# The product with w_co as seven block products instead of one full product, in an encoder layer

## The chip, the cores and the metric

The kernel runs on one NeuronCore of one Trainium2 chip. The metric is device time in microseconds (us) of one execution. Below, TensorE, VectorE (DVE), ScalarE (ACT), GpSimd (POOL) and SyncE (SP, which issues the DMAs here) are the core's engines.

## The reference

One layer of an encoder, in float32, for 1024 tokens of width 1024. Cut to what matters here:

```python
x = x + _rms_norm(mix, g_mix_post[l])
c = _memory_cross_attention(_rms_norm(x, g_cross_pre[l]), _rms_norm(mem, g_mem[l]), w_cq[l], w_ckv[l], w_co[l])
x = x + _rms_norm(c, g_cross_post[l])
f = _swiglu(_rms_norm(x, g_ffn_pre[l]), w_gate_up[l], w_down[l])
x = x + _rms_norm(f, g_ffn_post[l])

def _memory_cross_attention(h, mem_n, w_q, w_kv, w_o):
    # q (1024 tokens), k and v (256 memory tokens), 4 heads of 256
    p = jax.nn.softmax(jnp.einsum('bqhd,bkhd->bhqk', q, k) * (CROSS_HEAD_DIM ** -0.5), axis=-1)
    o = jnp.einsum('bhqk,bkhd->bqhd', p, v).reshape(b, s, D_MODEL).astype(h.dtype)
    return o @ w_o
```

The product of the change is `o @ w_o`: (1024 x 1024) times (1024 x 1024), with w_o called w_co in the kernel.

## The kernel before

Every float32 product is made of three matmuls on float32r operands: `split` (line 100) casts a value to a high part on ScalarE and subtracts that from the value on VectorE to get a low part (on GpSimd where `eng=nc.gpsimd`), and high x high, high x low and low x high are summed in PSUM. `load_w` (line 119) brings 512 KB of weights by DMA from SyncE's queue and splits them.

The kernel is written for a framework that sets the order of instructions on each engine's queue when the program is built. It takes instructions by priority, which is the order in which they are written, as far as its own estimate has them ready; work under `high_priority(AHEAD)` (AHEAD = 300) counts as written earlier. A pool hands out its buffers in the order written, and a tile's buffer is given on when its last reader is done. On the chip each queue then runs in its order.

PSUM has eight banks of 128 x 512 float32: in this part of the kernel four in pool pg, two in pn, two in px. Tokens are worked in two halves of 512 (hf 0 and 1), channels in 8 tiles of 128 (KT = 8).

The work around the change, in the order written:

1. `cross_q(hf)` (line 1116) makes the queries of a half, eight tiles of 24 matmuls in pg banks (tile pcq, line 261). `cross_attention(q)` (line 1125) goes over four heads. A head takes: the scores in two px banks (pcs, line 1137), their maximum (cmx, line 1139), the exponential (cpr, line 1144), the division by the sum (line 1147), eight transposes into two pn banks (pct, line 1153) and their split (cph, cpl), and the output in two px banks again (pco, line 1163), which is split in place over the queries. The order written is cross_q(0), cross_attention(q0), cross_q(1), cross_attention(q1).
2. `mid_gemm` (line 1034) multiplies a half by w_co: two halves of the columns, in each four loads of two weight tiles, and 96 matmuls of 512 columns over four pg banks (pmg, line 1052); 384 in all for the two halves of tokens. From each bank ScalarE takes the sum of squares (line 1055), VectorE multiplies by the gain (z, line 1056). Then come, for each of four tiles of 128 tokens, the norm's factor on GpSimd (lines 1064 and 1065), the residual (line 1066), the store to d_x2, the next norm's sum of squares and scaling (lines 1069 to 1075).
3. The scaled rows of the first half are transposed (`turned_k`, line 1191, tile ptn) and split into X11 and X21 (lines 1197 to 1200, raw copy xraw at line 1199). Those of the second half give the sums T1 to T4 and X22 (lines 1202 to 1218) for the gate/up product, which is made of seven block products in the kernel before too (as is the down projection, `block_product` at line 1400, tiles pdA, pdX, pdD).
4. The first EARLY = 4 pairs of gate/up tiles are multiplied with X11 and X21 alone (lines 1238 to 1254), while the second half is normed and transposed.

## Time and profile before

| | |
|---|---|
| time, median of 3 runs | 1535.4 us (1531.97 to 1537.91) |
| profiled execution | 1532.85 us, its span in the trace 1530.3 us |
| TensorE busy | 1484.3 us, 97% of the span |
| VectorE, ScalarE, GpSimd busy | 1068.5, 732.5, 391.2 us |
| granted TensorE clock, mean | 0.995 |

The profile is one execution. A row of groups gives line, engine, operation, output and inputs, shapes and count, then times. PE is TensorE's matmuls, PEld its weight loads. A matmul's duration in a row overlaps with its neighbours; the rate is read from long stretches. In a table of windows the columns are the window, its length, and the busy time and count of PE, PEld, DVE, ACT and (where it worked) POOL, then the granted TensorE clock, the DMA share and GB/s.

### The profile page before, as it was taken

Reading aid. Unit: us, or ns where it says so; the run is one execution under the profiler, and the core shown is the slowest. Engines: PE = TensorE matmul, PEld = TensorE weight load, DVE = VectorE, ACT = ScalarE, POOL = GpSimd, SP = SyncE. Lnnn points to the kernel's source line nnn. Section 1 sums busy time; section 2 is a strip of 40 time slices with the busy share of each in tenths; the row PEclk is TensorE's granted clock in tenths of the full one; section 3 lists DMA queues with packets and bytes.
Section 4 is the critical chain, followed back from the end, with each engine's and each line's share of the span. In section 5 each row is a group of like instructions: output and inputs, shape, how many; then the busy total and the mean of one; then the engine's idle time right before and its main releaser. Section 6 shows DMA issues by size and latency. Waiting matters only on the chain.

```text
span 1530.3 us, 21039 instructions
## 1 busy us (share of the span) xinstructions
PE 1484.3 (97%) x7451; PEld 1247.2 (81%) x7451; DVE 1068.5 (70%) x1716; ACT 732.5 (48%) x1494; POOL 391.2 (26%) x404
## 2 busy tenths in 40 slices
PE   6999999999899899999999999999999999999997
PEld 5888888877899778888887787888888888888786
DVE  6868999687789865524456387777877555696665
ACT  5678821447467664554336574323233333354532
POOL 2020221311236203243102232343434332000021
PEclk9999999999999999999999999999999999999999
DMA  6235575856997684453213354343433334853355
GB/s 208 76 108 149 145 194 150 217 167 176 313 315 221 200 280 155 150 168 106 76 54 132 111 192 131 125 137 116 160 124 104 103 104 168 291 178 98 104 177 167
DMA packets 264709, 242.95 MB, mean 159 GB/s; under 512 B 33800, under 2 KB 203677, under 8 KB 264605
## 3 DMA queue, kind: packets, MB, share of 16 engines
q1 hardware_dynamic: 264605, 241.62, 50.4%
q8 instruction: 58, 0.95, 0.3%
q14 instruction: 46, 0.38, 0.1%
HBM read 172.07 MB, written 66.88 MB: 156 GB/s over the span
## 4 chain that ended last, share of the span: by engine, by line
PE 75%; DVE 10%; DMA 6%; ACT 4%; issue 2%; SPq 2%; POOL 1%; DVEq 0%; POOLq 0%; ACTq 0%
PE pmg L1052 10%; PE pD L1231 8%; PE pE L1231 8%; PE pA L1231 7%; PE pcq L261 6%; PE pdX L1421 6%; PE pg L261 5%; PE pdA L1421 4%; PE pB L1231 4%; PE psc L809 3%; PE pdX L1514 2%; PE pdD L1421 2%; DVE acc L286 2%; PE pcs L1137 1%; PE pco L1163 1%
## 5 line engine op out<-in xcount | busy, mean ns | idle before, releaser
L103 ACT CAST whi<-wraw 128x1024 fp32r<-128x1024 f32 x108 | 113.4, 1051 | 160.5 <-PE pmg L1052 34.4
L261 PE MATMUL pg<-hhi,whi 128*128 128x512 f32 x352 | 139.3, 396 | 0.0
L261 PE MATMUL pg<-hlo,whi 128*128 128x512 f32 x352 | 139.3, 396 | 0.0
L261 PE MATMUL pg<-hhi,wlo 128*128 128x512 f32 x352 | 138.3, 393 | 0.0
L104 POOL TENSOR_TENSOR wlo<-wraw,whi 128x1024 fp32r<-128x1024 f32 x38 | 91.8, 2415 | 178.7 <-ACT whi L103 178.7
L104 DVE TENSOR_TENSOR wlo<-wraw,whi 128x1024 fp32r<-128x1024 f32 x70 | 88.6, 1266 | 69.8 <-ACT whi L103 65.8
L1052 PE MATMUL pmg<-whi,b 128*128 128x512 f32 x384 | 119.2, 394 | 0.4 <-ACT b L103 0.4
L1231 PE MATMUL pA<-s,whi 128*128 128x512 f32 x352 | 109.4, 392 | 1.0 <-ACT m L1248 1.0
L1052 PEld LDWEIGHTS pmg<-whi,b 128*128 128x128 f32 x384 | 71.4, 188 | 15.4 <-ACT b L103 1.3
L1421 PE MATMUL pdX<-dhl,whi 128*128 128x512 f32 x264 | 76.1, 390 | 1.5 <-DVE zv L1476 0.7
L1231 PEld LDWEIGHTS pA<-s,whi 128*128 128x128 f32 x352 | 65.5, 188 | 14.7 <-ACT m L1248 1.5
L261 PEld LDWEIGHTS pg<-hhi,whi 128*128 128x128 f32 x352 | 66.4, 189 | 13.4 <-ACT hhi L103 0.2
L261 PEld LDWEIGHTS pg<-hhi,wlo 128*128 128x128 f32 x352 | 66.5, 189 | 12.8
L261 PEld LDWEIGHTS pg<-hlo,whi 128*128 128x128 f32 x352 | 66.3, 188 | 12.8
L1308 POOL TENSOR_TENSOR act<-act,up 128x512 f32<-128x512 f32 x33 | 50.1, 1517 | 89.6 <-DVE up L1307 53.1
L1052 PE MATMUL pmg<-wlo,b 128*128 128x512 f32 x192 | 71.9, 391 | 0.0
L103 ACT CAST whi<-araw 128x1024 fp32r<-128x1024 f32 (+1 forms) x36 | 35.3, 981 | 71.3 <-PE pdX L1421 27.6
L1231 PE MATMUL pA<-s,wlo 128*128 128x512 f32 x176 | 68.7, 391 | 0.1
L104 DVE TENSOR_TENSOR wlo<-araw,whi 128x1024 fp32r<-128x1024 f32 (+1 forms) x36 | 40.8, 1132 | 38.9 <-ACT whi L103 38.8
L286 DVE SCALAR_TENSOR_TENSOR acc<-cp,cols,acc 128x1024 f32<-128x1024 f32 x48 | 62.0, 1293 | 0.1
L1280 POOL TENSOR_TENSOR sr<-wraw 128x512 f32<-128x512 f32 x22 | 30.0, 1362 | 125.2 <-DMA wraw<-in_w_gate_up_dram 125.2
L1451 POOL TENSOR_SCALAR frs<-sq 128x1 f32<-128x1 f32 x8 | 12.0, 1498 | 195.4 <-ACT jk L1440 194.5
(415 smaller groups left out, 4113.1 us busy)
## 6 DMA issues: line engine op xcount, KB each, us to landing
wraw<-in_w_gate_up_dram SPq DMA_DIRECT2D x52, 512.0 KB, 3.8
kv<-d_kv SPq DMA_DIRECT2D x32, 512.0 KB, 7.4
wraw<-in_w_in_dram SPq DMA_DIRECT2D x22, 512.0 KB, 4.5
b<-in_w_down_dram SPq DMA_DIRECT2D x20, 512.0 KB, 7.3
araw<-d_as SPq DMA_DIRECT2D x20, 512.0 KB, 3.9
pz<-d_pz SPq DMA_DIRECT2D x32, 256.0 KB, 6.7
wraw<-in_w_ckv_dram SPq DMA_DIRECT2D x16, 512.0 KB, 5.4
wraw<-in_w_out_dram SPq DMA_DIRECT2D x16, 512.0 KB, 3.7
```

What stands on the lines that cost most here:

```text
L103: nc.scalar.copy(hi, src)
L104: (eng or nc.vector).tensor_tensor(lo, src, f32(hi), ALU.subtract)
L261: nc.tensor.matmul(p_, w[:, k, :], ah[a][:, k, :], start=(k == 0 and i == 0), stop=(k == nk - 1 and i == 2))
L286: nc.vector.scalar_tensor_tensor(acc, cp[:, t:t + S], taps[t], acc, ALU.mult, ALU.add)
L809: nc.tensor.matmul(out[:, d, h, :], lt[:, d, h, :], rt[:, d, h, :], start=True, stop=True)
L1052: nc.tensor.matmul(pp[t], act[a][:, k, tt], w_[:, kk, :], start=(k == 0 and i == 0), stop=(k == KT - 1 and i == 2))
L1137: nc.tensor.matmul(pp[:, t2_, :], q[a][:, ct, tt], kr_[b_][:, ct, :], start=(j == 0 and i == 0), stop=(j == 1 and i == 2))
L1231: nc.tensor.matmul(out_, w[a][:, k, :], xx[b_][:, k, :], start=(start and k == 0 and i == 0), stop=(k == HK - 1 and i == 2), skip_group_ch ...
L1280: nc.gpsimd.tensor_tensor(s[0], b_[:, 0:HK], b_[:, HK:], ALU.add)
L1308: nc.gpsimd.tensor_tensor(o_, o_, up, ALU.mult)
L1421: nc.tensor.matmul(banks[t], a[:, k - k0, tt], w, start=(first and k == 0 and i == 0), stop=(k == NB - 1 and i == 2), skip_group_check=not ...
L1514: nc.tensor.matmul(X[t], a[:, k], w[:, k0 + k], start=False, stop=(k0 + k == NB - 1 and i == 2), skip_group_check=True)
```

## The change

With the attention's outputs (tokens by channels) in blocks A11, A12 (first half of tokens, first and second half of channels), A21, A22 (second half of tokens) and w_co in blocks B11, B12, B21, B22, the product is made of seven block products, each of 4 x 4 x 3 = 48 matmuls:

- A11 B11 and A12 B21, whose sum is the first half's left columns; the first is also kept as p1;
- S2 (B22 - B12 + B11), S1 (B12 - B11), S4 B22 and S3 (B22 - B12), and A22 (B21 - (B22 - B12 + B11)),

with S1 = A21 + A22, S2 = S1 - A11, S3 = A11 - A21, S4 = A12 - S2. The other three blocks of the result are sums of p1 and these on VectorE. The sums of weights are made on GpSimd (`minus`), those of attention outputs on VectorE out of the output banks, with float32 copies of the first half's outputs (raw) made by ScalarE. The first two products, S4's weights and the loads of blocks (`load_block`) use 14 loads of 512 KB. Products A11 B11, A12 B21, S4, S3 and A22 use pg banks, S2 and S1 the two px and the two pn banks. The norm of the first rows (`finish`) is written beside S3's product, their transposes after A22's; the buffers of several tiles move.

The core of the diff; left out are the pools' places, the transposes' sources and the names of X22's buffer:

```diff
-    def cross_attention(q):
+    def cross_attention(q, hf):
         for h in range(4):
             prs = []
             mxs = tx.tile([P, 4], F32, tag="cmx", name="cmx")
@@ -1162,47 +1167,199 @@
                     for i, (a, b_) in enumerate(((0, 0), (0, 1), (1, 0))):
                         nc.tensor.matmul(po, vr_[a][:, kt, cs], pts[kt][b_], start=(kt == 0 and i == 0),
                                          stop=(kt == 1 and i == 2))
-                split(q[0][:, 2 * h + j, :], q[1][:, 2 * h + j, :], po)
+                ct = 2 * h + j
+                if hf == 0:
+                    nc.scalar.copy(raw[:, ct], po)
+                    split(q[0][:, ct, :], q[1][:, ct, :], po)
+                    continue
+                k = ct % (KT // 2)
+                if ct < KT // 2:
+                    nc.scalar.copy(s1_[:, k], po)
+                    d_ = rg.tile([P, HALF], F32, tag="wpart", name="cs3", bufs=7)
+                    nc.vector.tensor_tensor(d_, raw[:, k], po, ALU.subtract)
+                    split(q[0][:, k], q[1][:, k], d_)
+                    continue
+                split(q[0][:, ct, :], q[1][:, ct, :], po)
+                nc.vector.tensor_tensor(s1_[:, k], s1_[:, k], po, ALU.add)
+                nc.vector.tensor_tensor(raw[:, k], s1_[:, k], raw[:, k], ALU.subtract)
+                nc.vector.tensor_tensor(raw[:, ct], raw[:, ct], raw[:, k], ALU.subtract)
 
     q0 = cross_q(0)
-    cross_attention(q0)
+    cross_attention(q0, 0)
     q1 = cross_q(1)
-    cross_attention(q1)
+    HK = KT // 2
+    wco = [opA.tile([P, KT, HALF], F32, tag=f"s0{i}", name="wco") for i in range(2)]
+    (b1_, b12), (b2_, p1_) = ((t[:, 0:HK], t[:, HK:KT]) for t in wco)
+
+    def load_block(b_, i, j):
+        for k0 in (0, 2):
+            nc.sync.dma_start(b_[:, k0:k0 + 2], w_co[(HK * i + k0) * P:(HK * i + k0 + 2) * P, j * HALF:(j + 1) * HALF]
+                              .rearrange("(k p) n -> p k n", p=P))
+
+    for b_, i, j in ((b12, 0, 1), (b1_, 0, 0), (b2_, 1, 1)):
+        load_block(b_, i, j)
+    cross_attention(q1, 1)
...
+    def weight_part(b_, k):
+        with tc.high_priority(AHEAD):
+            dh, dl = (rg.tile([P, HALF], F32R, tag="wpart", name="wpart", bufs=7) for _ in range(2))
+            split(dh, dl, b_[:, k])
+        return dh, dl
+
+    def act_part(a, k0):
+        if isinstance(a, tuple):
+            return [h[:, k0:k0 + 2] for h in a]
+        with tc.high_priority(AHEAD):
+            ah, al = (wp.tile([P, 2, HALF], F32R, tag=t, name=t) for t in ("whi", "wlo"))
+            split(ah, al, a[:, k0:k0 + 2])
+        return ah, al
+
+    def three(bank, ah, al, dh, dl, tt, start, stop, check):
+        for i, (a, w) in enumerate(((ah, dh), (ah, dl), (al, dh))):
+            nc.tensor.matmul(bank, a[:, tt], w, start=(start and i == 0), stop=(stop and i == 2), skip_group_check=not check)
+
+    def block_product(banks, a, b_, first=True, last=True, extra=None):
+
+        for k in range(HK):
+            if k % 2 == 0:
+                ah, al = act_part(a, k)
+            if isinstance(b_, tuple):
+                if k % 2 == 0:
+                    wh, wl = load_w(w_co[(HK * b_[0] + k) * P:(HK * b_[0] + k + 2) * P, HALF * b_[1]:HALF * (b_[1] + 1)], 2, HALF)
+                dh, dl = wh[:, k % 2], wl[:, k % 2]
+            else:
+                dh, dl = weight_part(b_, k)
+            for t in range(4):
+                three(banks[t], ah[:, k % 2], al[:, k % 2], dh, dl, slice(t * P, (t + 1) * P), first and k == 0,
+                      last and k == HK - 1, first and last)
+            if extra:
+                extra(k)
+
+    def minus(o_, a, b_):
+        nc.gpsimd.tensor_tensor(o_, a, b_, ALU.subtract)
+
+    def square_of(src, ch, r):
+        jk = tz.tile([P, D], F32, tag="junk", name="junk")[:, 0:src.shape[-1]]
+        nc.scalar.activation(jk, src, AF.Square, accum_out=ssq[:, ch, r:r + 1])
+
+    def finish(r, parts, eng):
+
+        tok = slice(r * P, (r + 1) * P)
+        xr = tz.tile([P, D], F32, tag="xr", name="xr", bufs=2)
+        nc.sync.dma_start(xr, d_x1[tok, :])
+        rs = tz.tile([P, 1], F32, tag="prs", name="prs", bufs=4)
+        nc.gpsimd.tensor_scalar(rs, ssq[:, 1, r:r + 1], ssq[:, 0, r:r + 1], D * EPS, ALU.add, ALU.add)
+        nc.gpsimd.tensor_tensor(rs, rs, mhalf[:, 0:1], ALU.pow)
+        for z, o_ in parts:
+            c_ = slice(o_, o_ + z.shape[-1])
+            nc.vector.scalar_tensor_tensor(xr[:, c_], z, rs, xr[:, c_], ALU.mult, ALU.add)
+        nc.sync.dma_start(d_x2[tok, :], xr)
+        s2 = tz.tile([P, 1], F32, tag="ps2", name="ps2", bufs=4)
+        jk = tz.tile([P, D], F32, tag="junk", name="junk")
+        nc.scalar.activation(jk, xr, AF.Square, accum_out=s2)
+        r2 = tz.tile([P, 1], F32, tag="pr2", name="pr2", bufs=4)
+        rstd_of(r2, s2, 1.0 / D, EPS)
+        for z, o_ in parts:
+            c_ = slice(o_, o_ + z.shape[-1])
+            if eng is nc.scalar:
+                nc.scalar.activation(z, xr[:, c_], AF.Identity, scale=r2)
+            else:
+                nc.vector.tensor_scalar(z, xr[:, c_], r2, None, ALU.mult)
+
+    a11, a12, s3_, a22 = ((q_[0][:, c], q_[1][:, c]) for q_ in (q0, q1) for c in (slice(0, HK), slice(HK, KT)))
+    s2_, s4_ = blocks(raw)
+
+    def four(spec):
+        return [p_.tile([P, HALF], F32, tag=t_, name="pst") for p_, t_ in spec]
+
+    def sums(k):
+        minus(b1_[:, k], b12[:, k], b1_[:, k])
+        minus(b12[:, k], b2_[:, k], b12[:, k])
+        minus(b2_[:, k], b2_[:, k], b1_[:, k])
+
+    A = four([PG] * 4)
+    block_product(A, a11, (0, 0), last=False)
+    for t in range(4):
+        nc.scalar.copy(p1_[:, t], A[t])
+    block_product(A, a12, (1, 0), first=False, extra=sums)
+    X = four([PX] * 2 + [PN] * 2)
+    block_product(X, s2_, b2_, last=False)
+    for t in range(4):
+        nc.scalar.activation(zz[:, t, 0:HALF], A[t], AF.Square, accum_out=ssq[:, 0, t:t + 1])
+        nc.vector.tensor_tensor(zz[:, t, 0:HALF], A[t], gp[:, 0:HALF], ALU.mult)
+    Y = four([PG] * 4)
+    block_product(Y, s4_, (1, 1))
+    for t in range(4):
+        nc.vector.tensor_tensor(zv[:, t], p1_[:, t], X[t], ALU.add)
+    block_product(X, s1_, b1_, first=False)
+    load_block(b1_, 1, 0)
+    for t in range(4):
+        nc.vector.tensor_tensor(zz[:, t, HALF:], p1_[:, t], Y[t], ALU.add)
+    for t in range(4):
+        nc.vector.tensor_tensor(zz[:, t, HALF:], zz[:, t, HALF:], X[t], ALU.add)
+        nc.vector.tensor_tensor(za[:, t], p1_[:, t], X[t], ALU.add)
+        square_of(zz[:, t, HALF:], 1, t)
+    Y = four([PG] * 4)
+    block_product(Y, s3_, b12, last=False, extra=lambda k: minus(b1_[:, k], b1_[:, k], b2_[:, k]))
+    for t in range(4):
+        nc.vector.tensor_tensor(zz[:, t, HALF:], zz[:, t, HALF:], gp[:, HALF:], ALU.mult)
+        finish(t, [(zz[:, t], 0)], nc.scalar)
+    for t in range(4):
+        nc.vector.tensor_tensor(za[:, t], za[:, t], Y[t], ALU.add)
+        square_of(za[:, t], 1, 4 + t)
+        nc.vector.tensor_tensor(za[:, t], za[:, t], gp[:, HALF:], ALU.mult)
+    acts = [act_part(a22, k0) for k0 in (0, 2)]
+    wts = [weight_part(b1_, k) for k in range(HK)]
+    for t in range(4):
+        for k in range(HK):
+            ah, al = (h[:, k % 2] for h in acts[k // 2])
+            three(Y[t], ah, al, *wts[k], slice(t * P, (t + 1) * P), False, k == HK - 1, False)
+        nc.vector.tensor_tensor(zv[:, t], zv[:, t], Y[t], ALU.add)
+        square_of(zv[:, t], 0, 4 + t)
+        nc.vector.tensor_tensor(zv[:, t], zv[:, t], gp[:, 0:HALF], ALU.mult)
+        finish(4 + t, [(zv[:, t], 0), (za[:, t], HALF)], nc.vector)
...
```

More of the change, by code (lines that the diff above doesn't have):

```diff
@@ L1175, in tile_hybrid_block @@
     opC = LX.enter_context(pool("opC", 1))
-    X22 = [opC.tile([P, KT // 2, HALF], F32R, name=f"x22{i}") for i in range(2)]
+    zz = opC.tile([P, 4, D], F32, tag="x22", name="zz")
     L3 = ExitStack()
-    tr = L3.enter_context(pool("tr", 1))
-    raw = tr.tile([P, KT, HALF], F32, name="xraw")
-    tz = L3.enter_context(pool("tz2", 1, side="right"))
+    tz = L3.enter_context(pool("tz2", 1))
     gp = gpost_tile(tz, g_cross_post)
-    HK = KT // 2
+    za, zv = (tz.tile([P, 4, HALF], F32, name=n) for n in ("za", "zv"))
@@ L1184, in blocks @@
+    ssq = tz.tile([P, 2, NT], F32, name="ssq")
     def blocks(t):
         return t[:, 0:HK], t[:, HK:KT]
[L1187 to L1188 removed]
+    def weight_part(b_, k):
[10 more added lines that the diff above has]
+        return ah, al
@@ L1203, in tile_hybrid_block @@
+    T2, T4 = (blocks(t) for t in operand(opA, "s0"))
     T1, T3 = (blocks(t) for t in operand(opB, "s2"))
+    X22 = opC.tile([P, 2, HK, HALF], F32R, tag="x22", name="x22")
+    X22 = [X22[:, i] for i in range(2)]
     for k in range(HK):
-        p0, p1 = turned_k(xn, k), turned_k(xn, k + HK)
+        p0, p1 = turned_k(last_rows, k), turned_k(last_rows, k + HK)
         g0, g1 = gain("ffn", k), gain("ffn", k + HK)
```

25 lines of the change are left out of this document (17 added, 8 removed).

## The prediction

> **What bounds the kernel now.** I read the page's engine totals and its chain first, then windows around the product with w_co, then single rows of the cross-attention beside it.
>
> ```profile
> PE 1484.3 (97%) x7451; PEld 1247.2 (81%) x7451; DVE 1068.5 (70%) x1716; ACT 732.5 (48%) x1494; POOL 391.2 (26%) x404
> ```
> ```profile
> PE 75%; DVE 10%; DMA 6%; ACT 4%; issue 2%; SPq 2%; POOL 1%; DVEq 0%; POOLq 0%; ACTq 0%
> ```
>
> TensorE is busy 97% of the span and is three quarters of the chain that ended last. A busy share alone says little of matmuls that overlap, so the rate comes next, from the chain in order of time: a stretch of the down projection, which already runs as seven block products.
>
> ```profile
> 1370.48 29.92 PE pdD L1421 x132
> ```
>
> A 512-column matmul costs 29.92/132 = 0.2267 us when nothing interrupts. A matmul removed is worth 0.2267 us only where TensorE has no other wait, so the idle time around the change decides. From the windows (the second column is the length, the third TensorE's busy time):
>
> ```profile
> 777.80:853.00 75.20, 72.61 (x378) 60.55 (x378) 43.24 (x69) 38.56 (x86) 9.81 (x16) 1.00 0.26 91
> ...
> 853.00:943.00 90.00, 87.19 (x406) 70.34 (x405) 60.02 (x78) 53.75 (x94) 25.34 (x26) 1.00 0.49 164
> ```
>
> The first window is the second half's cross-attention, the second is the rest of the w_co stage with the early gate/up products. TensorE idles 2.59 us in the one and 2.81 us in the other. So the w_co matmuls are paid in full, and there are only 5.4 us of waits for the change to remove. Why does an attention that is a chain of small steps leave TensorE busy? The windows of the w_co product alone (tile pmg) answer:
>
> ```profile
> 686.50:777.80 91.30, 17.62 (x72) 13.30 (x72) 0.00 (x0) 0.00 (x0) 1.00 0.30 95
> 777.80:853.00 75.20, 47.12 (x193) 35.41 (x194) 5.39 (x8) 5.39 (x16) 1.00 0.26 91
> 853.00:884.00 31.00, 29.05 (x120) 21.88 (x120) 4.00 (x6) 4.76 (x15) 1.00 0.42 136
> ```
>
> Of the 384 matmuls, 72 lie beside the first half's attention and 193 beside the second half's. They are the cover of the attention.
>
> **The change, term by term.** Removed: 384 matmuls become 7 x 4 x 4 x 3 = 336. That is 48 x 0.2267 = 10.9 us less on a full TensorE.
>
> Now the cover. The first two products (a11, a12) need only the first half's attention outputs, and they are 96 matmuls. Before, all 192 of the first half and those of the second half's finished heads could be used. The products with s2, s4 and s1 need all of the second half but for a part: the first half of s4's product (24 matmuls) after the third head. X's banks are the attention's own px and pn. The rows of the heads:
>
> ```profile
> 738.49 3.04 PE L1137 MATMUL pcs<-kr,b 128*128 128x256 f32 x24
> ...
> 761.72 3.04 PE L1137 MATMUL pcs<-kr,b 128*128 128x256 f32 x24
> ...
> 779.06 1.59 PE L1137 MATMUL pcs<-kr,b 128*128 128x256 f32 x12
> ...
> 801.15 3.04 PE L1137 MATMUL pcs<-kr,b 128*128 128x256 f32 x24
> ...
> 807.25 0.69 DVE L1147 TENSOR_TENSOR cpr<-cpr,csum 128x512 f32<-128x512 f32 x1
> ...
> 832.47 1.03 PE L1153 MATMUL pct<-ident,cpr 128*128 128x128 f32 x8
> ...
> 839.23 1.59 PE L1137 MATMUL pcs<-kr,b 128*128 128x256 f32 x12
> ...
> 852.28 0.40 PE L1163 MATMUL pco<-cph,vr 128*128 128x512 f32 x1
> ```
>
> While cover lasts a head takes 17 to 23 us (738.49 to 761.72 to 779.06), as the queue's order has it. The last head, with little cover, takes 852.68 - 839.23 = 13.4 us. TensorE's own part of a head is 24 score matmuls (3.04), 8 transposes (1.03) and 12 output matmuls (12 x 0.2267 = 2.72), 6.8 us. The first half's attention is placed after the same query projections as before, so I take it to use the same 72 matmuls, now of the 96. For the second half's heads 24 are left, and the 24 of s4: 48 x 0.2267 = 10.9 us. Four heads take 4 x 13.4 = 53.6 us and hold 4 x 6.8 + 10.9 = 38.1 us of work: 15.5 us idle where 2.6 us stood, +12.9 us. Bounds: heads of 11.5 us with their steps closer, or 14.5 us with more queued behind them: +6 to +18 us.
>
> Extra readers of the attention's output banks. Each bank is now also copied (first half, ScalarE) or added (second half's last two heads, VectorE) before the next head's scores may take it:
>
> ```profile
> L103 ACT CAST b<-pco x16: 568/587/593, 709.5 to 852.7; 128x512 fp32r<-128x512 f32 x16
> L104 DVE TENSOR_TENSOR b<-pco,b x16: 680/691/692, 710.1 to 853.5; 128x512 fp32r<-128x512 f32 x16
> ```
>
> One of a head's two banks is on the way to the next head: 4 x 0.587 + 2 x 0.691 = 3.7 us. In the first half this is not idle time but cover spent early, which is missing later. Bounds: 0 if the queue hides it, 7.5 us for both banks.
>
> The end of the attention. X may start when the last output bank is free: cast, subtraction, addition, 0.587 + 2 x 0.691 = 2.0 us. Bounds: 0, if s4's 24 matmuls are kept for it, and 6 us with three more subtractions and the split of s2.
>
> The clock. This case's trace has one place where TensorE waits a little in the middle of work:
>
> ```profile
> 535.93 0.38 PE L654 MATMUL psw<-khi,qs 128*128 128x256 f32 x1 [2.15 <-DVE m L656]
> ```
> ```profile
> 536.00:538.00 2.00, 1.66 (x9) 1.32 (x10) 1.80 (x7) 0.97 (x3) 0.20 (x1) 0.73 1.03 388
> 538.00:540.00 2.00, 2.00 (x9) 1.52 (x7) 0.58 (x3) 2.00 (x10) 0.00 (x0) 0.50 1.05 395
> 540.00:542.00 2.00, 1.77 (x7) 1.04 (x7) 1.91 (x7) 1.96 (x4) 0.00 (x0) 0.92 1.07 376
> ```
>
> After 2.15 us of idle the granted clock was 0.73, 0.50 and 0.92 in three stretches of 2 us, which loses 2 x (0.27 + 0.50 + 0.08) = 1.7 us of full speed. A naked head has one longer gap, from the last score matmul (804.19) to the end of the softmax (807.94), 3.75 us. Two of the four heads stay without cover in it: 2 x 1.7 = 3.4 us; bounds 0 and 13.6 us (two gaps in every head).
>
> [...]
>
> After the attention. Five products, TensorE has 4 x 48 + 24 matmuls, 49 us, and beside them stand many reads of banks and splits:
>
> ```profile
> L1056 DVE TENSOR_TENSOR z<-pmg,gpost x32: 676/684/693, 575.5 to 886.2; 128x512 f32<-128x512 f32 x32
> ```
> ```profile
> L104 DVE TENSOR_TENSOR wlo<-wraw,whi 128x1024 fp32r<-128x1024 f32 x70 | 88.6, 1266 | 69.8 <-ACT whi L103 65.8
> ...
> L1280 POOL TENSOR_TENSOR sr<-wraw 128x512 f32<-128x512 f32 x22 | 30.0, 1362 | 125.2 <-DMA wraw<-in_w_gate_up_dram 125.2
> ...
> wraw<-in_w_out_dram SPq DMA_DIRECT2D x16, 512.0 KB, 3.7
> ```
> ```profile
> 812.82 1.28 DVE L1066 SCALAR_TENSOR_TENSOR z<-z,prs,xr 128x1024 f32<-128x1024 f32 x1 [0.36 <-POOL prs L1065]
> ...
> 817.40 1.14 ACT L1075 ACTIVATE xr<-z,pr 128x1024 f32<-128x1024 f32 x1
> ```
> ```profile
> L1199 ACT ACTIVATE xraw<-ptn,cols x8: 689/701/735, 853.2 to 868.7; 128x512 f32<-128x512 f32 x8
> ```
>
> VectorE: 32 operations on banks and sums and 16 weight splits at 0.69 (33 us), 8 splits at 1.27 (10 us), four residual updates at 1.28 (5 us): 48 us in 49 us, if none is done ahead. It is nearly full. The first rows' norm and turning, before under the last 120 matmuls, now start when s1's product ends, under 96 (21.8 us). In the old rows the residual update to the scaled row is 818.54 - 812.82 = 5.7 us, three more tiles two ScalarE passes of about 1.14 us each, 6.8 us, and the turning 15.5 us from 853.2 to 868.7, of which the early gate/up products need the first half before they start: 5.7 + 6.8 + 7.8 = 20 us at best, 28 us for all. I take 3 us, bounds 0 and 8 us.
>
> Hidden: the twelve and four weight subtractions on GpSimd (16 x 1.36 = 22 us) lie beside the attention, where GpSimd has 9.81 us of work in 75; without that cover s2's product would wait for them. The w_co loads are 14 of 512 KB instead of 16; the six that now stand on SP's queue ahead of the second attention wait for the end of the query projection, and take 6 x 3.7 = 22 us at most, where s2's product comes a whole attention (53.6 us) later. The eight fp32 copies of the first half and four of the second are on ScalarE, busy 38.56 of 75.20 us; their part on the banks is counted above. The last rows' norm goes on under the same early products as before, at no change.
>
> Sum: -10.9 + 12.9 + 3.7 + 2.0 + 3.4 + 3 = +14.1 us. The profiled execution took 1532.85 us (span 1530.3), so 1547.0 us for it; on the median of the three runs, 1535.4 us, it is 1549.5 us, the forecast. Half a percent, about what a measurement of this kernel can tell from no change, is 7.7 us: 1527.7 and 1543.1.
>
> **The rivals.** *The cover lasts.* If the queue's order spends fewer matmuls on the first half's heads, with three of them at 17.3 us (the step 761.72 to 779.06) instead of 23.2, 18 us of the 96 matmuls' cover move to the second half and the 15.5 us of idle time vanish, the clock term with them. What is left is -10.9 - 2.6 + 3.7 + 2.0 and nothing after: -7.8, 1528 us; 1524 if the banks cost nothing. For it: 17.3 occurred. Against: the same projections lie beside the same heads, and the 72 matmuls were spent there. It decides when the idle time of the whole stage stays under 8.6 us (5.4 + 10.9 - 7.7).
>
> *Half covered.* If also X's part on the two pn banks fills the last heads (12 to 24 matmuls, 2.7 to 5.4 us) and the clock stays up, +14.1 - 5.4 - 3.4 = +5.3, 1541 us. For it: pn is free once the last head is transposed. Against: X's px half waits for the last bank.
>
> *The clock falls in every head.* Two gaps in each of four heads: 8 x 1.7 instead of 3.4, +24.3 us, 1560 us. For it: the wait for the transposed probabilities' split is a second gap. Against: that split's first part should take about the 0.59 us of the same cast on an output bank.
>
> *VectorE bounds the five products.* The 8 us bound in place of 3, with 6 at the attention's end: +23.1, 1558.5 us. Against: loads of weights and b2's splits can be done in the attention.
>
> **How the numbers follow.** Forecast 0.46 (its own range 1540 to 1562), cover lasts 0.22, half covered 0.16, clock 0.09, VectorE 0.07. Faster by over 0.5%: 0.20, nearly all of the first rival. Within: 0.24, half covered, a tail of the forecast and the first rival's weaker end. Slower: 0.56, the rest. The range 1526 to 1570 leaves out the best end of the first rival (0.08) and sums where several upper bounds meet (0.1).
>
> **What would show it.** The w_co product has 336 matmuls. Right: the second half's heads come every 12 to 15 us and TensorE idles 12 to 20 us in them, with the granted clock under 1.00 there; the first output product is finished before the third of these heads; the last products run at 0.2267 us with under 6 us of waits. Wrong: heads of 17 us and more with TensorE full to the end of the attention (then it is faster), or idle time mostly behind the attention, named by VectorE.

## The result, and the profile after

The changed kernel takes 1579.5 us (median of 4 runs, 1577.3 to 1583.1), the kernel before 1536.5 us in the same comparison: 1.0287 times as long, 95% interval 1.0255 to 1.0320. That is 43 us more where the forecast was 14 more. It was slower, as forecast, but by three times as much.

The profiled execution of the changed kernel took 1581.4 us, its span is 1579.7 us. Its page, engine totals and the chain that ended last:

```profile
PE 1491.0 (94%) x7403; PEld 1245.9 (79%) x7403; DVE 1108.9 (70%) x1776; ACT 747.2 (47%) x1522; POOL 414.6 (26%) x420
```
```profile
PE 40%; DVE 1%; POOL 1%; ACT 1%; issue 0%; DVEq 0%; POOLq 0%; ACTq 0%
```

The 48 matmuls are gone (7403 instead of 7451), but TensorE is busy longer, 1491.0 us instead of 1484.3: the mean granted clock of this execution was 0.984, before 0.995. Its share fell from 97% to 94%. The chain, followed back from the end, now gets no further than the stage of the change.

The loss is all in one place. From the start to the first score matmul of the cross-attention (655.5 us before, 656.4 after) and from the first pB matmul (the early product that needs the last rows' sums) to the end (597.8 and 598.9 us) the two kernels agree. Between them I cut three stretches: the second half's attention (from 777.8 us in every run) up to its last output matmul, then the products up to the last w_co matmul, then the stretch from there to the first pB matmul, called the tail below. Windows of the kernel before (start and end, length, TensorE's busy time, then the other engines; the number ahead of the DMA share is the granted clock):

```profile
777.80:852.60 74.80, 72.22 (x374) 60.15 (x374) 43.10 (x68) 38.16 (x85) 9.81 (x16) 1.00 0.27 92
852.60:882.80 30.20, 30.20 (x148) 25.07 (x147) 10.90 (x13) 18.38 (x36) 12.19 (x13) 1.00 0.39 129
882.80:932.50 49.70, 48.62 (x226) 39.07 (x224) 43.65 (x58) 34.62 (x57) 13.16 (x14) 1.00 0.54 182
```

The same three stretches of the changed kernel:

```profile
777.80:837.60 59.80, 43.25 (x211) 33.94 (x210) 32.14 (x62) 23.17 (x60) 2.52 (x3) 0.89 0.00 1
837.60:909.00 71.40, 60.77 (x242) 46.71 (x241) 49.52 (x66) 33.80 (x57) 18.23 (x20) 0.93 0.35 118
909.00:980.80 71.80, 55.28 (x252) 43.04 (x250) 54.57 (x75) 45.98 (x83) 23.24 (x26) 0.92 0.46 154
```

The attention ends 15 us earlier, because fewer product matmuls lie in it. But the products behind it take 71.4 us, of which 240 x 0.2267 = 54.4 us are TensorE's own work, and the tail takes 71.8 us instead of 49.7. TensorE is idle 59.80 - 43.25 = 16.6, then 10.6 and 16.5 us: 43.7 us instead of 2.6 + 0 + 1.1 = 3.7. The granted clock, 1.00 before, is 0.89, 0.93 and 0.92; length times what is missing to 1 gives 6.6 + 5.0 + 5.7 = 17.3 us. That is an estimate, since it takes in the idle time too; by busy time it is 19.2 us (159.3 us instead of 151.0, with 10.9 us of work gone). Together: -10.9 + 40.0 + 17.3 = 46.4 us, against 203.0 - 154.7 = 48.3 us by the windows.

The table of waits says for whom TensorE waited (the changed kernel from 777.8 to 985 us: sum, times, longest, in us):

```profile
PE pct L1158 <- DVE cpr L1152: 10.9, 6, 3.9
PE pB L1388 <- ACT s1h L103: 8.6, 1, 8.6
PE pst L1233 <- ACT whi L103: 5.8, 4, 2.1
PE pst L1233 <- DVE wlo L104: 2.4, 3, 1.3
PE ptn L1343 <- DVE zv L1281: 2.4, 1, 2.4
PE ptn L1343 <- ACT zz L1279: 2.3, 1, 2.3
PE pcs L1142 <- DVE cs L1179: 1.9, 2, 0.9
...
PE pcs L1142 <- DVE os L1183: 1.5, 1, 1.5
```

The first is the wait for a head's softmax, now with nothing beneath it, the second the tail, the third and fourth the splits of the products' operands. The largest of the kernel before in the same place (777.8 to 935 us):

```profile
PE pA L1231 <- ACT m L1248: 1.0, 1, 1.0
```

### The profile page after: what moved, and what is told of

The parts are those of the page before. It is cut to its first block, busy times and chain, and to the rows that moved or that the text cites. A ratio compares the mean times of both kernels' runs of the same rounds, so it can differ in the third digit from the quotient of the medians.

```text
span 1579.7 us, 21087 instructions
## 1 busy us (share of the span) xinstructions
PE 1491.0 (94%) x7403; PEld 1245.9 (79%) x7403; DVE 1108.9 (70%) x1776; ACT 747.2 (47%) x1522; POOL 414.6 (26%) x420
## 5 line engine op out<-in xcount | busy, mean ns | idle before, releaser
L103 ACT CAST whi<-wraw 128x1024 fp32r<-128x1024 f32 x98 | 102.9, 1051 | 153.4 <-DMA wraw<-in_w_gate_up_dram 30.4
L1388 PE MATMUL pA<-b,whi 128*128 128x512 f32 x352 | 112.7, 400 | 3.5 <-ACT m L1405 1.9
L104 DVE TENSOR_TENSOR wlo<-wraw,whi 128x1024 fp32r<-128x1024 f32 x60 | 77.7, 1296 | 44.7 <-ACT whi L103 42.1
L1388 PEld LDWEIGHTS pA<-b,whi 128*128 128x128 f32 x352 | 66.4, 191 | 18.4 <-ACT m L1405 2.3
L261 PEld LDWEIGHTS pg<-hhi,wlo 128*128 128x128 f32 x352 | 66.2, 188 | 12.8
L261 PEld LDWEIGHTS pg<-hlo,whi 128*128 128x128 f32 x352 | 66.2, 188 | 12.8
L1388 PE MATMUL pA<-b,wlo 128*128 128x512 f32 x176 | 69.3, 394 | 0.0
L1388 PE MATMUL pB<-s,s1h 128*128 128x512 f32 x176 | 54.8, 393 | 8.6 <-ACT s1h L103 8.6
L1579 PEld LDWEIGHTS pdX<-dhl,whi 128*128 128x128 f32 x264 | 49.3, 188 | 12.8 <-ACT dhl L103 1.1
L103 ACT CAST dhl<-b 128x512 fp32r<-128x512 f32 x66 | 40.4, 620 | 33.5 <-PE pdA L1579 14.1
```

Of the source, the lines that this page charges most:

```text
L103: nc.scalar.copy(hi, src)
L104: (eng or nc.vector).tensor_tensor(lo, src, f32(hi), ALU.subtract)
L261: nc.tensor.matmul(p_, w[:, k, :], ah[a][:, k, :], start=(k == 0 and i == 0), stop=(k == nk - 1 and i == 2))
L1388: nc.tensor.matmul(out_, w[a][:, k, :], xx[b_][:, k, :], start=(start and k == 0 and i == 0), stop=(k == HK - 1 and i == 2), skip_group_ch ...
L1579: nc.tensor.matmul(banks[t], a[:, k - k0, tt], w, start=(first and k == 0 and i == 0), stop=(k == NB - 1 and i == 2), skip_group_check=not ...
```

## The experiments

Times are medians with their range. Each ratio is to the kernel before, run beside it (its medians there: 1535.4 for the first four, 1535.0 for the next four, 1536.0 for e9 to e12, 1532.9 for e13 and e14). The changed kernel's own ratio is 1.0287 [1.0255, 1.0320], so a change to it of under some 6 us can't be told from none. The windows and waits of a run are those of its one profiled execution.

**More cover, placed first (e1).** A11 x B11 is made twice:

```diff
     A = four([PG] * 4)
+    block_product(A, a11, (0, 0), last=False)
     block_product(A, a11, (0, 0), last=False)
```

> The changed kernel with the product of the blocks A11 and B11 made twice (the second time over the first): 48 more matmuls of 512 columns, 10.9 us at 0.2267 us each, that need only the first half's attention. Theory (the second half's attention has too little cover, and its waits let the clock fall): they go into waits that are there anyway, the time rises by 0 to 4 us or falls, and the second half's heads up to the second show TensorE full at clock 1.00. Rival (TensorE's own work bounds the stage): plus 10.9 us, ratio to the kernel before up by 0.007.

Measured: 1587.0 us (1585.6 to 1588.6), 1.0329 [1.0312, 1.0346]. That is 7 us more than the changed kernel for 10.9 us of added work, between the two expectations, and the intervals do not tell it from the whole 10.9. The last heads stayed bare: TensorE still waits 10.5 us for softmaxes in this attention (10.9 in the changed kernel), and its end moved out by 8 us.

**Four buffers for the residual rows (e2).** Each row from the third on gets memory of its own, in blocks that are dead by then:

```diff
-        xr = tz.tile([P, D], F32, tag="xr", name="xr", bufs=2)
+        if r < 2:
+            xr = tz.tile([P, D], F32, tag="xr", name="xr", bufs=2)
+        else:
+            xr = (s1_, b2_, b12)[r // 2 - 1][:, r % 2 * 2:r % 2 * 2 + 2].rearrange("p k n -> p (k n)")
```

> The changed kernel with no residual tile used again: rows 0 and 1 keep their two buffers, rows 2 to 7 take blocks that are dead by then (S1, the weight sums). Theory A (two residual buffers in turn hold up the norms of the rows, first the first rows' transposes, then the last rows', until the early gate/up products run out): 15 to 22 us faster, the wait of 8.6 us before the first product with T2 gone or under 2 us. Theory B (VectorE's and GpSimd's own work in that tail is the bound): under 4 us faster, the wait moves little.

Measured: 1582.3 us (1576.5 to 1584.5), 1.0292 [1.0266, 1.0318]: no change. The theory that the two row buffers by themselves set the tail fell.

**S4's product ahead of S2's (e3).** Two statements change places, so that S4's 48 matmuls, which need no bank of the attention, come first:

```diff
+    Y = four([PG] * 4)
+    block_product(Y, s4_, (1, 1))
     X = four([PX] * 2 + [PN] * 2)
     block_product(X, s2_, b2_, last=False)
...
-    Y = four([PG] * 4)
-    block_product(Y, s4_, (1, 1))
```

> The changed kernel with S4's product written before S2's. As it is, S4's splits take the two buffers of weight parts behind those of S2's second half, which is ready only at the attention's end, so its first 24 matmuls covered nothing. Theory (order of the buffers): 24 matmuls of S4 lie before the attention's end and the time falls by 4 to 8 us. Rival (S4's sums are ready too late or VectorE is full): within 2 us.

Measured: 1582.6 us (1578.9 to 1584.8), 1.0298 [1.0277, 1.0318]: no change. S4's product did not move beneath the attention. TensorE's waits in this run have a new line:

```profile
PE pst L1233 <- DVE zz L1301: 6.2, 1, 6.2
```

S4's pg banks hold the first output block. That is evacuated into zz with the gain, and by the order of the kernel's pools both lie in memory that comes free only when the attention is over.

**Low parts of the weight sums on GpSimd (e4).**

```diff
-            split(dh, dl, b_[:, k])
+            split(dh, dl, b_[:, k], eng=nc.gpsimd)
```

> The changed kernel with the low parts of the 16 weight-sum splits on GpSimd in place of VectorE: 16 x 0.69 = 11 us less on VectorE, 16 x 1.3 = 21 us more on GpSimd, which is nearly idle from the second half's attention to its end. Theory (VectorE bounds the five products and lengthens the heads): 4 to 8 us faster. Rival (TensorE waits there for the order of buffers and the clock): within 2 us, or slower by up to 5 us because each split takes twice as long.

Measured: 1580.7 us (1580.0 to 1584.1), 1.0286 [1.0268, 1.0304]. The products behind the attention took 67.0 us instead of 71.4, and the tail 75.0 instead of 71.8. The first of these is no sure gain: in e1, e5 and e7, where nothing of these five products was changed, they took 67.5 to 67.9 us. The expected 4 to 8 us did not come.

**A scratch tile of its own for the second sum of squares (e5), the same with e2 (e6).** The squares of `finish` no longer share the tile "junk" with those of `square_of`:

```diff
-        jk = tz.tile([P, D], F32, tag="junk", name="junk")
+        jk = p1_[:, r % 2 * 2:r % 2 * 2 + 2].rearrange("p k n -> p (k n)")
```

> The changed kernel with the scratch output of the second sum of squares of each row tile put in the dead block p1, so that the one buffer of the scratch tile is left to the first sums of squares. Theory (the buffer is handed out in the order written, so the square of row tile t+1's product waits for tile t's whole norm, and the last four tiles come 6 to 9 us apart where they came 1.5 us apart before): the last four scalings come within 12 us instead of 18.9, and the time falls by 6 to 15 us. Rival (the order on VectorE and GpSimd or the two residual buffers hold them as much): within 3 us.

> The changed kernel with both: the scratch in p1 and no residual tile used again. Theory (two chains of buffers in series, each hiding the other's removal): 12 to 20 us faster than the changed kernel, the 8.6 us wait before the first T2 product under 3 us. Rival (VectorE and GpSimd are the bound of that tail): under 5 us faster.

Measured: 1577.0 us (1573.0 to 1580.1), 1.0267 [1.0235, 1.0299], and 1577.0 us (1575.9 to 1578.4), 1.0268 [1.0238, 1.0299]: two or three us, which the intervals do not tell from none. But the two edits together did what neither did alone. The last four scalings lay 18.4 us apart, first to last start, in the changed kernel, 17.3 in e2 and 22.0 in e5 (12 were expected); in e6 they lie 6.0 us apart, close to the 5.4 of the kernel before. The first and the last of them:

```profile
924.24 1.49 DVE L1284 TENSOR_SCALAR zv<-wco,pr 128x512 f32<-128x512 f32 x1
...
930.22 1.50 DVE L1284 TENSOR_SCALAR zv<-wco,pr 128x512 f32<-128x512 f32 x1 [0.44 <-POOL pr L162]
```

So the row buffer and the scratch tile space the last rows, each of them enough by itself; and the spacing is not what sets the tail, which is 69.0 us long in e6 instead of 71.8. The sums T1 to T4 began 14 us earlier, but the first pB matmul came only 2.7 us earlier. TensorE's waits of e6 from 900 to 985 us, the first two:

```profile
PE ptn L1346 <- DVE zv L1284: 6.8, 1, 6.8
PE pB L1391 <- ACT s1h L103: 2.0, 1, 2.0
```

The wait for pB fell from 8.6 to 2.0 us, and one of 6.8 us for the last rows' scaled values stands in its place: their transposes are ahead of early products on TensorE's queue.

**The cover spread over the heads (e7), and e2, e5 and e7 together (e8).** Groups of the first two products are held behind the scores of later heads; a pair in `hold` names the half and the head, one for each of a product's four groups:

```diff
+                if hold and hold[k]:
+                    order_.enter_context(tc.issue_after(last_score[hold[k]].ins))
...
-    block_product(A, a11, (0, 0), last=False)
+    block_product(A, a11, (0, 0), last=False, hold=(None, None, (1, 0), (1, 0)))
...
-    block_product(A, a12, (1, 0), first=False, extra=sums)
+    block_product(A, a12, (1, 0), first=False, extra=sums, hold=((1, 1), (1, 1), (1, 2), (1, 3)))
```

> The changed kernel with the matmuls of A11 B11 and A12 B21 held back: 24 free, 24 behind the scores of the second half's first head, 24 behind the second's, 12 behind the third's and 12 behind the fourth's. The number of matmuls is the same. Theory (the cover is spent in the first half's heads, and each naked head idles about 4 to 6 us and lets the clock fall): TensorE's idle time in the second half's attention falls from 16.7 us to under 9, the clock stays at 1.00 there, the time falls by 7 to 14 us. Rival (the first half's last head loses as much as the others gain): within 3 us.

> The changed kernel with the scratch in p1, no residual tile used again, and the cover held back. If attention and tail are separate losses, the gains add: 20 to 32 us faster than the changed kernel, 1548 to 1560 us. If the time lost is one shared bound (VectorE over the whole stage), the sum is much less than the parts: under 12 us.

Measured: e7 1579.2 us (1575.5 to 1581.3), 1.0280 [1.0252, 1.0308]; e8 1574.2 us (1571.0 to 1576.7), 1.0249 [1.0221, 1.0277]. In e7 the waits in the attention did shrink and its clock stayed at 1.00 (below, under the hardware), and the last w_co matmul came 6.8 us earlier. But the profiled execution was e7's fastest, 1575.5 us, and the median did not move. All three together won at most some 5 us where 20 to 32 were expected if attention and tail were separate losses; the interval overlaps with the changed kernel's. Mending the changed kernel wait by wait does not find the loss. The next runs test the order of the work.

**The kernel before in the changed kernel's order (e9).** The full product, no block sums; only the first half's first columns lie beneath the second attention, and the first rows' result is whole 96 matmuls ahead of the last rows'. In `chunk` the arguments are the operand, the half of the rows, the half of the columns, the banks, and the matmul behind which it is held:

```diff
-    xn = mid_gemm(tz, q0, w_co, gp, d_x1, d_x2, 0)
+    chunk(q0, 0, 0, [PG] * 4)
+    chunk(q1, 1, 0, [PX] * 2 + [PN] * 2)
+    chunk(q0, 0, 1, [PG] * 4, last_pco)
+    xn = norm_rows(0)
+    chunk(q1, 1, 1, [PG] * 4)
...
-    xn = mid_gemm(tz, q1, w_co, gp, d_x1, d_x2, 1, vec=True)
+    xn = norm_rows(1)
```

> The kernel before, with the full product and no block sums, but in the order of the changed kernel: only the first half's first 512 columns (96 matmuls) are made beneath the second half's attention; the second half's first columns, the first half's last columns and the second half's last columns follow it, so that the first rows' result is whole 96 matmuls before the last rows' instead of about 240. Theory (the loss comes from giving up the stagger of the two halves): the second attention ends 10 to 16 us earlier, the stretch from the last product matmul to the first early product grows from 49.7 to 60 or more, and the kernel takes 1565 to 1590 us. Rival (the loss comes from the extra sums, splits and bank readers of the seven products): only the missing cover in the attention is felt, that stretch stays at 47 to 53 us, and the kernel takes 1545 to 1555 us.

Measured: 1568.1 us (1566.4 to 1571.5), 1.0209 [1.0180, 1.0238]. The order, with the banks and buffers that it needs (px and pn banks for one block, the last rows' block in the later memory of X22) and none of the change's arithmetic, costs 32 us. The three stretches:

```profile
777.80:837.40 59.60, 45.42 (x226) 35.29 (x225) 28.25 (x54) 21.00 (x59) 0.00 (x0) 0.91 0.05 18
837.40:900.70 63.30, 63.30 (x283) 52.40 (x282) 26.52 (x28) 28.40 (x47) 11.74 (x21) 1.00 0.47 156
900.70:966.30 65.60, 55.55 (x253) 43.22 (x251) 48.22 (x59) 43.52 (x73) 23.00 (x22) 0.95 0.41 135
```

The attention and the tail look like those of the changed kernel (14.2 and 10.1 us idle). The products do not: with the full product TensorE is busy all of 63.3 us at full clock. The longest of TensorE's waits from 895 to 970 us are for the first rows' splits and raw copies (s, xraw) and for a weight split:

```profile
PE pA L1286 <- POOL s L104: 2.3, 2, 2.1
PE pA L1286 <- ACT whi L103: 2.1, 1, 2.1
PE ptn L1247 <- ACT xraw L1252: 1.9, 1, 1.9
```

**Only the cover taken away (e13).** The kernel before, its order kept, but the first half's last columns held behind the attention:

```diff
+                    if ch and hold is not None:
+                        order_.enter_context(tc.issue_after(hold.ins))
...
-    xn = mid_gemm(tz, q0, w_co, gp, d_x1, d_x2, 0)
+    xn = mid_gemm(tz, q0, w_co, gp, d_x1, d_x2, 0, hold=last_pco)
```

> The kernel before, with the full product, where the first half's last 512 columns (96 matmuls) are held behind the second half's last attention output and everything else keeps its order: the cover in the attention is that of the changed kernel (96 matmuls), but the first rows' result is still whole 192 matmuls before the last rows'. It parts the 32 us of the run without the stagger into the missing cover and the nearness of the two results. If the missing cover alone costs them: 1564 to 1572 us. If the nearness of the two norms counts by itself: the attention's idle time and lowered clock stay (about 14 and 5 us), the stretch from the last product to the first early product is back at 50 to 55 us, and the kernel takes 1550 to 1560 us.

Measured: 1554.4 us (1551.9 to 1558.4), 1.0137 [1.0106, 1.0167].

```profile
777.80:837.60 59.80, 47.04 (x210) 36.23 (x209) 28.51 (x54) 20.62 (x59) 0.00 (x0) 0.80 0.06 18
837.60:908.50 70.90, 69.82 (x322) 57.45 (x321) 26.80 (x28) 36.99 (x63) 22.55 (x29) 1.00 0.41 141
908.50:958.10 49.60, 48.51 (x226) 39.11 (x225) 43.52 (x58) 34.55 (x57) 13.11 (x14) 1.00 0.52 176
```

The attention still lacks its cover (12.8 us idle, clock 0.80), but with 192 matmuls between the two results the tail is 49.6 us, that of the kernel before (49.7). So e13 and e9 part the 32 us: some 21 for the missing cover, lowered clock included, some 11 for two results that come close together (by the two intervals 5 to 17).

**Norms left out of the changed kernel (e10, e11, e14).** `finish` is taken out for the last rows, for the first rows, or for both, and a store of the columns with their gain stands in its place, so these kernels leave out the norm, the residual and its load.

> The changed kernel with the last rows' norm and residual left out (their scaled columns are stored and turned as they are); the products, the bank sums and the first rows' norm stay. Theory (the stretch after the last product is set by the last rows' norm, whose rows follow each other at 6 to 7 us): 15 to 22 us less, 1557 to 1564 us. Rival (the first rows' turning and its splits set that stretch): 0 to 5 us less, 1574 to 1579 us.

> The changed kernel with the first rows' norm and residual left out (their scaled columns are stored and turned as they are); the last rows' norm stays. Theory (two norms at the same time hold each other up on VectorE, ScalarE and GpSimd): the last rows follow each other at 2 to 3 us, 10 to 20 us less, 1559 to 1569 us. Rival (the last rows' own chain is what takes the time, alone as well): 0 to 5 us less, 1574 to 1579 us.

> The changed kernel with both norms and residuals left out (all scaled columns are stored and turned as they are); products and bank sums stay. If the two norms hold each other up and nothing else: the gains of the two runs with one norm left out (8.2 and 13.9 us) add up or more, 1550 to 1558 us. If behind them the next wait is as long (bank sums, turning): 1560 to 1567 us.

Measured: 1571.3 us (1566.6 to 1572.0), 1565.6 us (1564.0 to 1570.1) and 1561.8 us (1560.9 to 1562.6); ratios 1.0220 [1.0195, 1.0246], 1.0195 [1.0169, 1.0220], 1.0182 [1.0152, 1.0211]. Without the last norm 8 us are won and without the first 14, the one between its two expectations, the other in the theory's; without both it is no more than 18, the second expectation. The tail goes from 71.8 us to 61.3, 60.3 and 53.0 us. The windows of e14:

```profile
777.80:843.30 65.50, 49.20 (x229) 38.66 (x228) 34.36 (x65) 23.82 (x62) 5.83 (x4) 0.84 0.03 9
843.30:909.10 65.80, 58.23 (x259) 45.70 (x258) 46.34 (x64) 32.20 (x60) 12.88 (x8) 1.00 0.31 104
909.10:962.10 53.00, 49.54 (x234) 39.78 (x233) 41.64 (x57) 34.74 (x60) 8.67 (x6) 1.00 0.45 147
```

(The first score matmul of e14 came 3.5 us later than the changed kernel's, so its first stretch begins that much earlier in the work.) Without norms the tail is nearly that of the kernel before: each norm taken out shortens it by about 10 us. But the kernel before has the last rows' norm in its tail of 49.7 us too. With that norm alone, in e11, the tail is still 60.3 us, 10.6 us longer, with the first rows' transposes and splits left in it. So a second norm is about half of what lengthens the tail; the rest these runs do not part. What still costs in e14 is the attention (16.3 us idle) and the products (7.6 us). One part of the theory fell: the slow last rows were read as held up by the first rows' norm. Scaling of the last rows, in the kernel before, in the changed one, and in e11 (four operations; first and last start):

```profile
L1073 DVE TENSOR_SCALAR xr<-z,pr x4: 752/753/756, 888.5 to 893.9; 128x1024 f32<-128x1024 f32 x4
```
```profile
L1281 DVE TENSOR_SCALAR zv<-xr,pr x4: 483/489/496, 923.2 to 941.6; 128x512 f32<-128x512 f32 x4
```
```profile
L1281 DVE TENSOR_SCALAR zv<-xr,pr x4: 486/488/489, 919.6 to 937.3; 128x512 f32<-128x512 f32 x4
```

They are spread over 5.4, 18.4 and 17.7 us. Without the first norm the rows follow each other no faster, so the other norm is not what spaces them. It is the row buffer and the scratch tile, either of them enough (e2, e5 and e6).

**No low parts for the sums (e12).** The high part is used in their place, in as many matmuls; the same edit stands in `act_part`.

```diff
...
-            split(dh, dl, b_[:, k])
-        return dh, dl
+            nc.scalar.copy(dh, b_[:, k])
+        return dh, dh
...
```

> The changed kernel with no low parts made for the summed operands (the high part stands in for the low one, in as many matmuls): VectorE loses 32 subtractions and their waits. Theory (splits on VectorE stand between the products, which take 71.4 us after the attention where TensorE's own work is 54.4): the products take 60 to 65 us, and the kernel is 5 to 10 us faster, 1569 to 1574 us. Rival (the waits there are for bank readers, and what is won is given back behind): the kernel is within 3 us of the changed one, 1576 to 1582 us.

Measured: 1584.0 us (1579.9 to 1585.7), 1.0306 [1.0280, 1.0331]. The products behind the attention take 64.5 us instead of 71.4, as expected, and the tail 81.0 instead of 71.8: all of it is given back, as the rival had it (the time lies 2 us above its range). Taking work off VectorE, here and in e4, did not shorten the kernel.

## Why the prediction was wrong

The runs in a row part the 43 us as follows (medians, each against the kernel before beside it): +21.5 for the attention's missing cover (e13), +10.6 for the two results close together (e9 less e13), and +10.9 from e9 to the changed kernel. By the intervals the last two are known to about 6 us each. The last step has 48 matmuls, 10.9 us, taken away in it, so the block sums, the splits and their readers cost some 21.8 us; that is a difference, and e4 and e12, which took some of that work off VectorE, did not win it back. Point by point:

1. *Removed, -10.9.* Right: 336 matmuls.
2. *The cover, +12.9.* Right in its place: 16.6 us idle in the attention instead of 2.6, +14.0, of which 3.4 us are point 3's. That leaves +10.6. The heads of the second half (their first score matmuls, and in brackets the waits for the banks and for the softmax):

```profile
781.48 1.59 PE L1142 MATMUL pcs<-kr,b 128*128 128x256 f32 x12
...
794.37 3.14 PE L1142 MATMUL pcs<-kr,b 128*128 128x256 f32 x24 [0.93 <-DVE cs L1179]
...
807.25 3.13 PE L1142 MATMUL pcs<-kr,b 128*128 128x256 f32 x24 [0.94 <-DVE cs L1179]
...
814.27 0.63 PE L1158 MATMUL pct<-ident,cpr 128*128 128x128 f32 x4 [3.89 <-DVE cpr L1152]
...
822.04 3.13 PE L1142 MATMUL pcs<-kr,b 128*128 128x256 f32 x24 [1.52 <-DVE os L1183]
...
829.04 2.29 PE L1158 MATMUL pct<-ident,cpr 128*128 128x128 f32 x8 [3.88 <-DVE cpr L1152]
```

They come every 12.9, 12.9 and 14.8 us, the last takes 15.6; forecast were 12 to 15. That the idle time came out so near is in part luck. S4's first 24 matmuls, which the prediction gave to the last heads, came only behind the attention, at 855 us, for the reason that e3 showed. The heads took 56.1 us instead of 53.6, and in them TensorE was busy for 40.3 us (forecast 38.1) without S4's 5.4 us, at a clock of 0.88.

Nor is all of it missing cover. In e13 the last three heads, as bare, wait 1.7 us each for their softmax; here the third and the fourth wait 3.9 us, since VectorE has other work ahead of the scores' maximum (cmx). In the fourth head that is the block sums of S2 and S4 (oraw):

```profile
823.10 1.28 DVE L1184 TENSOR_TENSOR oraw<-os,oraw 128x512 f32<-128x512 f32 x2
824.30 0.68 DVE L1144 TENSOR_REDUCE cmx<-pcs 128x2 f32<-128x512 f32 x1
...
824.90 1.28 DVE L1185 TENSOR_TENSOR oraw<-oraw 128x512 f32<-128x512 f32 x2
826.10 0.68 DVE L1144 TENSOR_REDUCE cmx<-pcs 128x2 f32<-128x512 f32 x1
```

The prediction had VectorE's sums and splits on the output banks and behind the attention, not in the softmax.

3. *Readers of the output banks, +3.7.* Near in size: the waits of the scores (pcs) for the new readers of their banks (cs, os) sum to 3.4 us. But e13, without these readers, has waits of 1.8 us in the same place (pcs for b, shown at the end), so not all of the 3.4 us is the readers' own.
4. *End of the attention, +2.0.* The size was right, the cause was not: X started before the last output bank was free, and the one long wait, 2.1 us, comes 7 us after the attention's end, for the split of s2, which the prediction had in its upper bound only:

```profile
844.65 2.56 PE L1233 MATMUL pst<-wpart,whi 128*128 128x512 f32 x8 [2.13 <-ACT whi L103]
```

5. *The clock, +3.4.* This term was too small by a factor of five: 17.3 us by the windows. The prediction priced two gaps of the attention, where 6.6 us were lost, inside its bound of 13.6. The other 10.7 us were lost in the products and the tail, where it had no gaps to price; all three stretches, each with gaps, ran below full clock (0.89, 0.93 and 0.92).
6. *After the attention, +3, bounds 0 and 8.* Too small: 10.6 us idle in the products, 8.5 without the 2.1 us of point 4. VectorE's work was as forecast, 49.5 us busy for 48, but it did not bound the products. TensorE waited for splits of operands, and ScalarE, which makes their high parts, had itself waited for TensorE to leave the tile (a line of the table of waits of all engines; all four waits lie between 837.6 and 909 us):

```profile
ACT whi L103 <- PE pst L1233: 18.1, 4, 6.7
```

So a cast stood idle until a buffer came free, and then the next product waited for the cast. Whether more buffers for these tiles would have helped was not tested. No rival named this, though "VectorE bounds the five products" was the nearest.
7. *"The last rows' norm goes on under the same early products as before, at no change."* This step failed outright. The tail has 16.5 us of idle time where it had 1.1, and a clock of 0.92 beside, before 1.00. The prediction looked at each norm's cover (96 matmuls for the first rows, the early products for the last rows) and saw that each had some. It didn't see that the first rows' norm and turning, 28 us by its own sum, no longer end before the last rows' begin. Before, the first rows' residual was updated at 812.8 us, 70 us ahead of the last w_co matmul, and their turning (853 to 869 us) was over before that matmul. In the changed kernel the first rows' transposes end 10.6 us behind the last w_co matmul (909.0 us), when the last rows' residuals have begun:

```profile
L1343 PE MATMUL ptn<-ident,zz x32: 270/272/330, 895.9 to 919.6; 128*128 128x128 f32 x32
```
```profile
L1269 DVE SCALAR_TENSOR_TENSOR xr<-zv,prs,xr x4: 744/1254/1776, 914.7 to 938.7; 128x512 f32<-128x512 f32 x4
```

In e9, with the full product and that order, the tail grows to 65.6 us; in e13, with the old order, it stays at 49.6.

Points 5, 6 and 7 were short by 13.9, 5.5 and 15.4 us, 34.8 us together, and points 2 to 4 were 2.5 us too long. That makes 32.3 of the 34.2 us between the sum of 14.1 and the 48.3 us of the profiled windows; the other 1.9 us lie in the estimate of the clock. That seven products need most of both halves before any result is whole is in the prediction (four of the five products need the second attention), but only as a loss of cover.

The rivals: "the cover lasts" was to decide below 8.6 us of idle time, and there were 43.7. "Half covered" let X's matmuls fill the last heads; the first came at 835.2 us, 2.4 us before the attention's end. "The clock falls in every head" named the clock, which made 14 of these 34 us, but in one of three places. Of the marks set in advance, heads of 12 to 15 us, 12 to 20 us idle in them, a clock under 1.00 and the first output product done before the third head (at 788 us) came true; the last products with under 6 us of waits did not. The mark for "wrong", idle time mostly behind the attention, did come true (27.1 of 43.7 us), named by ScalarE's splits more than by VectorE. The prediction priced the clock from one wait of 2.15 us. In e13 no wait of TensorE in the attention is over 1.7 us and the clock there is 0.80; in the changed kernel it was 0.66 and 0.50 behind the two waits of 3.9 us (815 to 820 and 830 to 835 us).

No version beat the kernel before. The best of the changed ones that leave nothing out, e8, takes 1.0249 times as long.

## What to carry to other kernels

A block product that saves an eighth of the matmuls makes each result wait for more of the operands. Before counting what it saves, write down when each result was whole and when it will be: work that was staggered by half the data (here a product, a norm and a turning under the other half's attention) may come together at the end, where less covers it. To test that without writing the block product, put the old kernel's work in the new order and time it: here that run alone showed three quarters of the loss. And two buffers that each hold up the same rows hide each other: mending one left the rows as far apart (17.3 us in e2, where they had been 18.4, and no closer in e5), mending both brought them together (6.0 us in e6), though here the time hardly moved.

## What the hardware showed that I had not expected

In these runs the granted clock can't be read off the length of single waits. TensorE's waits in the attention of e13 and of e7 (sum, times, longest; the first three lines of each), e13 first:

```profile
PE pct L1156 <- ACT cpr L1147: 5.0, 3, 1.7
PE pct L1156 <- DVE cpr L1150: 3.4, 4, 1.0
PE pcs L1140 <- DVE b L104: 1.8, 3, 0.6
```
```profile
PE pct L1160 <- DVE cpr L1154: 3.1, 4, 1.1
PE pco L1170 <- ACT cph L103: 2.7, 4, 1.3
PE pcs L1144 <- DVE cs L1181: 1.9, 2, 0.9
```

And the window of that stage in e7:

```profile
777.80:840.00 62.20, 51.56 (x270) 40.78 (x271) 36.79 (x70) 29.02 (x73) 2.83 (x3) 1.00 0.06 21
```

With no wait over 1.7 us, e13 had 12.8 us of idle time in 59.8 and a clock of 0.80, which costs nearly as much again (59.8 x 0.20 = 12.0 us, an estimate). e7 had 10.6 us of idle time in 62.2, waits of up to 1.5 us, and kept 1.00. The idle time of a stretch does not tell either. From 820 to 830 us e13 (first row) idled 2.25 us at a clock of 0.78, e7 2.86 us at 1.00:

```profile
820.00:830.00 10.00, 7.75 (x36) 6.10 (x36) 4.11 (x9) 2.90 (x9) 0.00 (x0) 0.78 0.00 0
820.00:830.00 10.00, 7.14 (x43) 5.66 (x41) 8.80 (x17) 4.17 (x11) 0.00 (x0) 1.00 0.00 0
```

What tips the clock the runs leave open. It also varied from run to run: the four runs of e13 had a mean clock of 0.987, 0.990, 0.993 and 0.995 and took 1558.4, 1556.2, 1552.6 and 1551.9 us.
